# A four-layer streaming encoder on one core: half of the heads' evictions on another engine, the pooling gate's read issued elsewhere, and the convolution's steps reordered

## The chip, the cores and the metric

The kernel runs on one core of a Trainium2 chip. The core has five engines with queues of their own: TensorE (PE in the profile; its weight loads are shown apart as PEld), VectorE (DVE), ScalarE (ACT), GpSimd (POOL) and SyncE (SP), which only issues transfers. PSUM holds what PE writes, in banks of 128 x 512 fp32. The metric is the device time of one execution in microseconds (us); the number quoted is the median of several runs.

## The reference

256 tokens of 1024 channels pass through four layers. Each layer is a token mixer and then an MLP; the mixer is latent attention (MLA) in layers 0 and 3, a convolution module in layer 1 and a pooling mixer in layer 2. All arrays are fp32. Cut to what matters here:

```python
for i in range(DEPTH):                       # 4
    mod = silu(c) @ ada_w[i] + ada_b[i]      # six rows of 1024: shift, scale, gate, twice
    sh_m, sc_m, gt_m, sh_f, sc_f, gt_f = split(mod, 6)
    h = rmsnorm(x, g[i, 0]) * (1 + sc_m) + sh_m
    y = mixer(h)                             # i % 3: 0 MLA, 1 convolution, 2 pooling
    x = x + gt_m * rmsnorm(y, g[i, 1])
    h = rmsnorm(x, g[i, 2]) * (1 + sc_f) + sh_f
    y = square(relu(h @ w1[i])) @ w2[i]      # 1024 -> 4096 -> 1024
    x = x + gt_f * rmsnorm(y, g[i, 3])

def conv(h):
    a = h @ w_pw1 + b_pw1                    # 1024 -> 2048
    u = a[:, :1024] * sigmoid(a[:, 1024:])
    u = causal_depthwise(u, w_dw) + b_dw     # width 31
    return silu(layernorm(u)) @ w_pw2 + b_pw2

def pool(h):                                 # four groups of 256 channels, windows 2, 4, 8, 16
    p = trailing_mean(h) - h
    return (p @ w (by group) + b) * scale
```

## The kernel before

**Tiles.** The tokens are two tiles of 128 (tile 0 and tile 1), the channels eight blocks of 128. The residual stream `xs` stays in SBUF. Every fp32 matrix product is made of three products of rounded parts, high x high, high x low and low x high. For weights `load` brings a raw tile by DMA (issued on SP), ScalarE casts it to `hi` (L173), and VectorE subtracts that from the raw tile, which gives `lo` (L174). The activations are split in the same way: the tile `hT` holds a high and a low plane of the transposed activations.

**Heads.** Between two sublayers stands one call of `boundary` (L536; called a head here). For each token tile it does the following. ScalarE sums the squares of the result `y` (L135), POOL forms the root (L119, L121), VectorE multiplies y by the gate's row `bc_g` (`y_scaled`, L528, giving v) and adds it to the residual (`residual`, L533). `squares` then sums the squares of the new xs on ScalarE (L135, tile ms), POOL forms that root r, and VectorE multiplies xs by the scale row `bc_a` to give `xa`. PE turns xa into hT. For tile 0 that is `transposed0`: ScalarE writes a diagonal `dg` of r (L403), PE adds the shift and multiplies with dg (L395, L409) into two banks of four channel blocks each, and `fill0(h)` empties each bank into the planes, by a cast on ScalarE (L573) and a subtraction on VectorE (L574). For tile 1 it is `transposed1`: xa already holds r (L420), PE transposes (L426), ScalarE and VectorE empty the banks (L429, L431). Between them stands `first(0)`, the first product of the next sublayer with tile 0 (`headblock`, L645); `turned` then does tile 1 and turns the block (L659), which ScalarE copies out first (L657 in the convolution, L728 in the MLP). There are eight heads: six fill planes in this way, the one ahead of the pooling mixer hands over tokens instead, and the last one only writes the output.

**Modulation.** The rows of `mod` are computed in the background, in units of one 1024 x 2048 piece of `ada_w`: `ada(n, vec)` does n units, either on PE (L271, tile adap) or, for those in `vec`, as sums on VectorE (L221, L223, tile acc) that `ada_flush` hands to PE at the end. Tables (`MIX`, `FF`) say how many units each step of a stage does. A finished row is written to DRAM (`stage`), and read back to all partitions by a DMA that POOL issues (`spread`, L331); `gate_row(i)` does that for the gate bc_g, `prep` for bc_a.

**Order.** SP issues in the order in which the program is written. The other engines are ordered by the tile scheduler. `line(eng, ins)` pins an instruction behind the one pinned before it on its engine, and `gate[eng]` names an instruction behind which later weight casts, low parts, adap products or DMA reads are placed, without a semaphore. `gate["free"]` counts how many loads may pass ahead of it.

**Convolution** (`conv`, L1107). In iteration m of eight, PE forms block m of the first projection (`colblock`), ScalarE the sigmoid (L1174), VectorE the gated product `up` (L1176). SP writes that to DRAM (`ud`, L1179) and reads it back spread over shifted rows (`spread_taps`, L1150, four reads, tile u). `taps` runs 32 small matmuls with diagonal weights (L1131, tile dw_ps), ScalarE empties them with the bias (`uc`, L1134), and PE turns the result into tokens (L1136, tile ctok). Blocks 0 to 5 are done inside the loop for both tiles at once; blocks 6 and 7 after it, with the tiles as the outer loop:

```python
            for t in range(NT):
                for p, dg in zip(pend, dgs):
                    taps(*p, dg, t * P, P)
```

Then come the norm of each tile on VectorE (L1204 to L1211), its transposes on PE (L1220), the swish on ScalarE (L1225), the split on VectorE (L1230, L1231) and the second projection (`rowblock`, L602 to L606).

**Pooling** (`pool`, L1265). The head gives it tokens of tile 0 (L1290, on VectorE); its first call of `early` makes the window means of tile 0 on PE (L1309), the second one the first half of the product (L1330). ScalarE and VectorE split the means (L1317, L1320). After the head come tile 0's low product, tile 1's means, the gate's row (`gate_row(i)`) and tile 1's product.

## Time and profile before

| | |
|---|---|
| median of three runs | 1166.6 us (1164.24 to 1167.7) |
| profiled execution, device time | 1165.46 us |
| its span in the trace | 1163.7 us |
| mean granted clock of TensorE | 0.985 of full speed |
| busy in that span: PE, PEld, DVE, ACT, POOL | 1116.9, 910.8, 860.2, 643.3, 55.8 us |
| instructions | 17551, of them 6682 matmuls |
| moved by DMA | 290.02 MB, 249 GB/s in the mean |

The span runs from the first to the last instruction of the profiled execution; the device time beside it is that of the same execution. A row of the trace names the line of the kernel, the engine, the operation, the tile written and those read. A number in square brackets is the time for which the engine stood still just before, with what released it. [...]

### The profile page before, as it was taken

To read this page: it belongs to the slowest core of one execution; us is meant where nothing else is said; L and a number is where in the kernel's file an instruction comes from. 1 tells how busy PE (TensorE), PEld (TensorE's weight loads), DVE (VectorE), ACT (ScalarE), POOL (GpSimd) and SP (SyncE) were. 2 spreads that over 40 slices of the span, in tenths; PEclk is the share of its full clock that TensorE was granted. 3 is DMA by queue.
4 is the path that set the end of the run, shared out by engine and by line. 5 is a ranking of instruction groups with operands and counts; after the bars stand their busy time and mean duration, and the time that the engine had idled before them with its cause. 6 is when DMAs were issued, how large, how long until landed. Compare 5 with 4: busy or idle time off the path is not lost.

```text
span 1163.7 us, 17551 instructions
## 1 busy us (share of the span) xinstructions
PE 1116.9 (96%) x6682; PEld 910.8 (78%) x6682; DVE 860.2 (74%) x1206; ACT 643.3 (55%) x1146; POOL 55.8 (5%) x129
## 2 busy tenths in 40 slices
PE   7899999999999989999999989999998899999997
PEld 4667778878877767888888768888877778888886
DVE  3789788889675656888876688888756986655554
ACT  3455566555654225655564555656556665655653
POOL 1000000000010001000000100000010001000000
PEclk8999999999999989999999989999998999999999
DMA  9877769987825894898877559988625522765650
GB/s 367 321 275 305 294 241 348 336 318 286 316 86 174 308 341 155 307 388 328 307 282 293 226 207 379 332 314 289 210 72 177 172 91 71 258 197 188 188 187 36
DMA packets 73388, 290.02 MB, mean 249 GB/s; under 512 B 9988, under 2 KB 15236, under 8 KB 61016
## 3 DMA queue, kind: packets, MB, share of 16 engines
q1 hardware_dynamic: 70488, 280.45, 66.5%
q0 software_dynamic: 2816, 8.46, 2.1%
q8 instruction: 52, 0.85, 0.3%
q14 instruction: 32, 0.26, 0.1%
HBM read 286.58 MB, written 2.29 MB: 248 GB/s over the span
## 4 chain that ended last, share of the span: by engine, by line
PE 79%; DVE 7%; DMA 6%; ACT 3%; issue 3%; POOL 2%; SPq 0%; POOLq 0%; DVEq 0%; ACTq 0%
PE h L671 19%; PE y L602 11%; PE y L605 11%; PE y L606 11%; PE h L674 10%; PE adap L271 2%; DMA raw<-in_w_pw_dram 2%; ACT junk L135 2%; PE dw_ps L1131 2%; PE s_ps L1043 1%; DVE lo L174 1%; PE h L645 1%; POOL r L121 1%; PE pw L625 1%; PE pw L619 1%
## 5 line engine op out<-in xcount | busy, mean ns | idle before, releaser
L174 DVE TENSOR_TENSOR lo<-raw,hi 128x1024 fp32r<-128x1024 f32 (+1 forms) x334 | 391.4, 1194 | 79.6 <-ACT hi L173 53.1
L173 ACT CAST hi<-raw 128x1024 fp32r<-128x1024 f32 (+1 forms) x334 | 333.8, 1029 | 67.4 <-PE y L606 32.1
L671 PE MATMUL h<-hT,hi 128*128 128x512 f32 x960 | 240.0, 391 | 0.0
L671 PEld LDWEIGHTS h<-hT,hi 128*128 128x128 f32 x960 | 175.9, 188 | 36.2 <-issue 2.5
L605 PE MATMUL y<-lo,gh 128*128 128x512 f32 x512 | 200.0, 391 | 0.1
L606 PE MATMUL y<-hi,gl 128*128 128x512 f32 x512 | 199.1, 390 | 0.0
L602 PE MATMUL y<-hi,gh 128*128 128x512 f32 x512 | 197.2, 393 | 1.4 <-ACT hi L173 1.4
L736 ACT COPY r<-h 128x256 f32<-128x256 f32 x120 | 44.6, 372 | 183.4 <-PE h L674 183.3
L674 PEld LDWEIGHTS h<-hT,lo 128*128 128x128 f32 x960 | 130.8, 190 | 11.5 <-issue 2.5
L223 DVE SCALAR_TENSOR_TENSOR acc<-araw,c_act,acc 128x1024 f32<-128x1024 f32 x110 | 135.8, 1280 | 0.6 <-DMA araw<-in_ada_w_dram 0.5
L674 PE MATMUL h<-hT,lo 128*128 128x256 f32 x960 | 135.0, 283 | 0.0
L606 PEld LDWEIGHTS y<-hi,gl 128*128 128x128 f32 x512 | 96.1, 188 | 21.0 <-DVE gl L742 0.6
L602 PEld LDWEIGHTS y<-hi,gh 128*128 128x128 f32 x512 | 95.6, 188 | 21.2 <-ACT hi L173 1.6
L605 PEld LDWEIGHTS y<-lo,gh 128*128 128x128 f32 x512 | 96.3, 188 | 20.3 <-issue 1.7
L737 DVE TENSOR_TENSOR r<-h,r 128x256 f32<-128x256 f32 x120 | 50.3, 421 | 44.6 <-ACT r L736 43.5
L742 DVE TENSOR_TENSOR gl<-r,gh 128x512 fp32r<-128x512 f32 x60 | 41.4, 691 | 39.5 <-ACT gh L741 39.1
L738 ACT ACTIVATE r<-r 128x512 f32<-128x512 f32 x60 | 38.0, 633 | 33.3 <-DVE r L737 33.0
L528 DVE TENSOR_TENSOR v<-y,bc_g 128x512 f32<-128x512 f32 x32 | 21.9, 688 | 27.0 <-ACT junk L135 20.3
L602 PE MATMUL y<-hi,hT 128*128 128x512 f32 x96 | 38.2, 399 | 1.3 <-DVE hT L1230 1.3
L739 ACT ACTIVATE r<-r 128x512 f32<-128x512 f32 x60 | 37.9, 632 | 1.6
L741 ACT CAST gh<-r 128x512 fp32r<-128x512 f32 x60 | 37.2, 621 | 1.7
L605 PE MATMUL y<-lo,hT 128*128 128x512 f32 x96 | 37.5, 391 | 0.0
(262 smaller groups left out, 1470.2 us busy)
## 6 DMA issues: line engine op xcount, KB each, us to landing
raw<-in_w_dram SPq DMA_DIRECT2D x256, 512.0 KB, 4.7
araw<-in_ada_w_dram SPq DMA_DIRECT2D x96, 1024.0 KB, 7.2
raw<-in_w_pw_dram SPq DMA_DIRECT2D x24, 512.0 KB, 7.5
raw<-in_w_o_dram SPq DMA_DIRECT2D x16, 512.0 KB, 4.4
u<-ud SPq DMA_DIRECT2D x32, 132.0 KB, 3.3
raw<-in_w_ukv_dram SPq DMA_DIRECT2D x8, 512.0 KB
bc_g<-rowd POOLq DMA_DIRECT2D x8, 512.0 KB, 4.2
bc_a<-rowd POOLq DMA_DIRECT2D x7, 512.0 KB, 8.0
```

Of the source, the lines that this page charges most:

```text
L173: put(A.copy(h, raw), "act")
L174: put(V.tensor_tensor(l, raw, h.bitcast(F32), op=ALU.subtract), "dve")
L223: V.scalar_tensor_tensor(acc, raw[:, sl], ck, acc, op0=ALU.mult, op1=ALU.add)
L602: mm = T.matmul(o, ah, bh, start=start, stop=False, skip_group_check=True)
L605: T.matmul(o, ah, bl, start=False, stop=False, skip_group_check=True)
L606: return T.matmul(o, al, bh, start=False, stop=stop, skip_group_check=True)
L671: T.matmul(b, w(0, kk), pair[:, :, kk], start=(kk == 0), stop=False, skip_group_check=True)
L674: T.matmul(b[:, 0:S], w(1, kk), pair[:, 0, kk], start=False, stop=(kk == KT - 1), skip_group_check=True)
L736: A.copy(rf, hb[:, S:])
L737: V.tensor_tensor(rf, hb[:, 0:S], rf, op=ALU.add)
L738: A.activation(r, r, AF.Relu)
L742: gli = V.tensor_tensor(gl, g2, gh.bitcast(F32), op=ALU.subtract)
```

## The change

- In the six heads that fill planes, `fill0(1)` casts on VectorE instead of ScalarE, and it is issued behind tile 1's residual, squares and root. Where the head does modulation units, the first half's low part is issued ahead of it.
- In the head before layer 2's MLP the low parts of the first weight block are `held`: they are placed behind `scaled(0)`.
- In the pooling stage `gate_row(i)` is called in the head's first call of `early`, where it stood behind tile 1's means.
- Modulation sums on VectorE are placed behind `gate["dve"]`.
- In the convolution the turnings of a block are collected and done in the middle of the next taps (`turn`), the reads of block m-1 are issued on SP ahead of block m's write, the last two blocks run with the block as the outer loop, `ada_flush` comes behind them, adap products are placed behind the latest tap matmul, casts from m = 2 on behind the copies of the head block, and `MIX[1]` has its units in another order.

```diff
-    def load(src, pre=None, lined=False):
+    def load(src, pre=None, lined=False, held=None):
...
-        put(V.tensor_tensor(l, raw, h.bitcast(F32), op=ALU.subtract), "dve")
+        def rest():
+            return V.tensor_tensor(l, raw, h.bitcast(F32), op=ALU.subtract)
+        if held is None:
+            put(rest(), "dve")
+        else:
+            held.append(lambda: line("dve", rest()))
...
+                    if gate["dve"] is not None:
+                        nosync(ins, gate["dve"])
...
             xa = scaled(0)
+            for h in held:
+                h()
...
         def fill0(h):
             o = (slice(None), slice(4 * h, 4 * h + 4), slice(0, P))
-            line("act", A.copy(planes[0][o], bs[h]))
+            if h == 0:
+                line("act", A.copy(planes[0][o], bs[h]))
+            else:
+                line("dve", V.tensor_copy(planes[0][o], bs[h]))
             return lambda: line("dve", V.tensor_tensor(
                 planes[1][o], bs[h], planes[0][o].bitcast(F32), op=ALU.subtract))
         if tokens is None:
-            low = [fill0(h) for h in range(2)]
+            low = [fill0(0)]
         residual(1, v1, r1)
...
         else:
+            if units:
+                low.pop(0)()
+            low.append(fill0(1))
             for l in low:
                 l()
...
+            turns = []
+
+            def turn():
+                for uc, m, c0, w in turns:
+                    for t in range(w // P):
+                        line("pe", T.transpose(
+                            ctok[c0 // P + t][m // 4][:, (m % 4) * P:(m % 4) * P + P],
+                            uc[:, t * P:(t + 1) * P], ident))
+                turns.clear()
...
                 for mm in range(8):
+                    if mm == 4:
+                        turn()
                     for q in range(4):
-                        T.matmul(b[32 * q:32 * q + 32, 0:w], dg[:, mm, q, :],
-                                 u4[:, q, mm + c0:mm + c0 + w], start=(mm == 0), stop=(mm == 7))
+                        gate["pe"] = line("pe", T.matmul(
+                            b[32 * q:32 * q + 32, 0:w], dg[:, mm, q, :],
+                            u4[:, q, mm + c0:mm + c0 + w], start=(mm == 0), stop=(mm == 7)))
...
-                for t in range(w // P):
-                    T.transpose(ctok[c0 // P + t][m // 4][:, (m % 4) * P:(m % 4) * P + P],
-                                uc[:, t * P:(t + 1) * P], ident)
+                turns.append((uc, m, c0, w))
...
-                    hb = turned(first, vp.tile([P, 512], F32, tag="uc", name="r0", bufs=2), A.copy)
+                    def put(rt, b):
+                        cpy.append(A.copy(rt, b))
+                    cpy = []
+                    hb = turned(first, vp.tile([P, 512], F32, tag="uc", name="r0", bufs=2), put)
+                    last.clear()
                 else:
+                    if m == 2:
+                        gate["act"] = cpy[1]
                     hb = colblock(w_pw1[j, m], hh, hl, "pw1")
...
+                if m > 0:
+                    pend.append(spread_taps(*uds.pop(0)))
                 ud = dr.tile([4, 32, 288], F32, tag="ud", name="ud")
                 nc.sync.dma_start(ud.rearrange("b r t -> (b r) t"), u)
                 uds.append((m, ud))
-                if m > 0:
-                    pend.append(spread_taps(*uds.pop(0)))
...
-            ada_flush()
...
-            for t in range(NT):
-                for p, dg in zip(pend, dgs):
+            for p, dg in zip(pend, dgs):
+                for t in range(NT):
                     taps(*p, dg, t * P, P)
+            turn()
+            ada_flush()
...
             if not spilt:
+                gate_row(i)
                 parts = [means(0, h) for h in range(2)]
...
         gate["free"] = 0
-        gate_row(i)
         prep(i, 2)
...
-        1: ([0, 0, 2, 1, 2, 1, 1, 0, 0], 1, 3),
+        1: ([0, 1, 2, 1, 2, 1, 0, 0, 0], 1, 3),
...
-                first = headblock(w1[i, 0] if m else w_pw1[i // 3, 0], hi, lo)
+                held = [] if m and i % 3 == 2 else None
+                first = headblock(w1[i, 0] if m else w_pw1[i // 3, 0], hi, lo, held)
```

The lines of the changed kernel differ: fill0's cast is L583 on ScalarE and L585 on VectorE, the low part L586, dg L410, the transposes' evictions L436, xa L427, the taps L1159, the turnings L1147, the write of ud L1214, the reads of u L1177.

**ScalarE in the head ahead of layer 1's MLP.** The squares with tile msy are those of y, with ms those of the new xs; dg is tile 0's diagonal; L573 (now L583) empties tile 0's banks, L429 (now L436) those of tile 1; L728 and L729 (now L743 and L744) begin the MLP's first block. Before:

```order
L135 ACTIVATE junk,msy<-y_4485 128x512
L403 ACTIVATE dg<-ident,r 128x128
L135 ACTIVATE junk,msy<-y_4486 128x512
L573 CAST hT<-hT_ps 128x4x128 x2
L135 ACTIVATE junk,ms<-xs 128x512 x2
L728 ACTIVATE r<-h_4709 128x256
L429 ACTIVATE hT<-hT_ps,shc 128x128 x4
```

and now:

```order
L135 ACTIVATE junk,msy<-y_4485 128x512
L410 ACTIVATE dg<-ident,r 128x128
L135 ACTIVATE junk,msy<-y_4486 128x512
L583 CAST hT<-hT_ps 128x4x128
L135 ACTIVATE junk,ms<-xs 128x512 x2
L743 ACTIVATE r<-h_4709 128x256
L436 ACTIVATE hT<-hT_ps,shc 128x128 x8
```

One of the two casts has left ScalarE, and the squares of tile 1's xs follow the first cast directly; the copy of the MLP's block now stands ahead of all of tile 1's evictions. On VectorE the second cast stands between the two low parts, behind tile 1's residual (L540) and ahead of xa.

**VectorE in the pooling stage,** from the split of the means on. L1320 (now L1354) is the low part of the means, L528 (now L535) y times the gate's row, L533 (now L540) the residual, L389 (now L396) xa of tile 0, L174 (now L175) the low part of a weight. Before:

```order
L1320 TENSOR_TENSOR hT<-pT_ps,hT 128x4x128
L528 TENSOR_TENSOR v<-y_6499,bc_g 128x512
L528 TENSOR_TENSOR v<-y_6500,bc_g 128x512
L1320 TENSOR_TENSOR hT<-pT_ps,hT 128x4x128 x2
L174 TENSOR_TENSOR lo<-raw,hi 128x1024 x2
L533 SCALAR_TENSOR_TENSOR xs<-v,r,xs 128x512 x2
L389 TENSOR_TENSOR xa<-xs,bc_a 128x512 x2
L528 TENSOR_TENSOR v<-y_6501,bc_g 128x512
```

and now:

```order
L1354 TENSOR_TENSOR hT<-pT_ps,hT 128x4x128
L535 TENSOR_TENSOR v<-y_6501,bc_g 128x512
L535 TENSOR_TENSOR v<-y_6502,bc_g 128x512
L540 SCALAR_TENSOR_TENSOR xs<-v,r,xs 128x512
L1354 TENSOR_TENSOR hT<-pT_ps,hT 128x4x128 x2
L540 SCALAR_TENSOR_TENSOR xs<-v,r,xs 128x512
L396 TENSOR_TENSOR xa<-xs,bc_a 128x512 x2
L175 TENSOR_TENSOR lo<-raw,hi 128x1024 x2
L535 TENSOR_TENSOR v<-y_6503,bc_g 128x512
```

The two weight low parts have moved behind tile 0's residual and xa, and the residual's halves stand around the low parts of tile 1's means.

**TensorE at the end of the convolution,** from block 6's taps for tile 0 on. The operand u_4192 (now u_4188) is block 6, u_4236 (now u_4234) block 7; ctok_3392 is the second channel half of tile 0's tokens, ctok_3394 that of tile 1. Before:

```order
L1131 MATMUL dw_ps<-u_4192,dg 32x128 x32
L1136 MATMUL ctok_3392<-ident,uc 128x128
L1131 MATMUL dw_ps<-u_4236,dg 32x128 x32
L1131 MATMUL dw_ps<-u_4192,dg 32x128 x5
L1136 MATMUL ctok_3392<-ident,uc 128x128
L1131 MATMUL dw_ps<-u_4192,dg 32x128 x27
L1131 MATMUL dw_ps<-u_4236,dg 32x128 x5
L1136 MATMUL ctok_3394<-ident,uc 128x128
L1131 MATMUL dw_ps<-u_4236,dg 32x128 x27
L1220 MATMUL sT_ps<-ident,un 128x128 x4
L1136 MATMUL ctok_3394<-ident,uc 128x128
```

and now:

```order
L1159 MATMUL dw_ps<-u_4188,dg 32x128 x32
L1147 MATMUL ctok_3392<-ident,uc 128x128
L1159 MATMUL dw_ps<-u_4188,dg 32x128 x16
L1159 MATMUL dw_ps<-u_4234,dg 32x128 x16
L1147 MATMUL ctok_3394<-ident,uc 128x128
L1159 MATMUL dw_ps<-u_4234,dg 32x128 x32
L1147 MATMUL ctok_3392<-ident,uc 128x128
L1159 MATMUL dw_ps<-u_4234,dg 32x128 x16
L278 MATMUL adap<-acc,ones_c 32x512 x3
L1147 MATMUL ctok_3394<-ident,uc 128x128
L278 MATMUL adap<-acc,ones_c 32x512
L1254 MATMUL sT_ps<-ident,un 128x128 x8
```

Tile 0's tokens were complete while 59 tap matmuls of tile 1 were still to come; they are now complete 16 tap matmuls before the taps end.

## Rows read from the trace of the kernel before

**Rows 1.** The page, part 1: busy time of each engine, share of span, instructions.
```profile
span 1163.7 us, 17551 instructions
PE 1116.9 (96%) x6682; PEld 910.8 (78%) x6682; DVE 860.2 (74%) x1206; ACT 643.3 (55%) x1146; POOL 55.8 (5%) x129
```
**Rows 2.** Waits of PE, whole span: who waits, on whom; us in total, times, longest.
```profile
PE hT_ps L426 <- DVE xa L420: 6.6, 11, 1.9
...
PE y L1330 <- DVE hT L1320: 2.9, 1, 2.9
PE ctok L1136 <- ACT uc L1134: 2.7, 5, 1.1
...
PE dw_ps L1131 <- DMA u<-ud: 2.0, 1, 2.0
...
PE gT L659 <- ACT r L657: 1.1, 1, 1.1
```
**Rows 3.** Windows: us, busy of PE, PEld, DVE, ACT, POOL, PEclk, DMA share, GB/s.
```profile
346.00:352.00 6.00, 4.87 (x42) 4.67 (x41) 5.98 (x14) 5.74 (x11) 0.55 (x1) 1.00 0.28 90
423.60:429.60 6.00, 5.42 (x93) 4.69 (x97) 0.00 (x0) 0.37 (x1) 0.00 (x0) 0.51 0.96 384
655.00:670.00 15.00, 12.62 (x100) 10.93 (x92) 7.20 (x12) 6.75 (x14) 3.38 (x7) 1.00 0.99 399
873.60:876.40 2.80, 2.78 (x12) 2.78 (x13) 1.54 (x6) 2.14 (x8) 0.55 (x1) 0.50 0.79 291
```
**Rows 4.** Timeline, head of layer 1's MLP: start, us, instruction, [wait before, releaser].
```profile
467.97 0.59 ACT L573 CAST hT<-hT_ps 128x512 fp32r<-128x512 f32 x1 [0.91 <-PE hT_ps L409]
468.45 0.64 ACT L135 ACTIVATE junk<-xs 128x512 bf16<-128x512 f32 x1
...
467.09 0.69 DVE L574 TENSOR_TENSOR hT<-hT_ps,hT 128x512 fp32r<-128x512 f32 x1 [0.81 <-ACT hT L573]
...
471.01 1.54 DVE L420 SCALAR_TENSOR_TENSOR xa<-xs,r,bc_a 128x256 f32<-128x256 f32 x3 [1.73 <-POOL r L121]
...
471.55 0.83 PE L426 MATMUL hT_ps<-ident,xa 128*128 128x128 f32 x4 [0.75 <-DVE xa L420]
```
**Rows 5.** Groups by line and form: busy us, mean ns of one, idle before, releaser.
```profile
L1067 DVE COPY ptA<-pT_ps 128x512 f32<-128x512 f32 x8 | 5.5, 691 | 2.3 <-PE pT_ps L1066 2.2
...
L573 ACT CAST hT<-hT_ps 128x512 fp32r<-128x512 f32 x12 | 7.0, 587 | 14.2 <-PE hT_ps L409 14.2
...
L223 DVE SCALAR_TENSOR_TENSOR acc<-araw,c_act,acc 128x1024 f32<-128x1024 f32 x110 | 135.8, 1280 | 0.6 <-DMA araw<-in_ada_w_dram 0.5
```
**Rows 6.** Timeline, pooling stage, columns as in rows 4.
```profile
654.82 0.68 DVE L528 TENSOR_TENSOR v<-y,bc_g 128x512 f32<-128x512 f32 x1
...
659.77 0.63 POOL L331 DMA_DIRECT2D bc_g<-rowd  x1
...
668.54 1.29 DVE L528 TENSOR_TENSOR v<-y,bc_g 128x512 f32<-128x512 f32 x2 [6.67 <-DMA bc_g<-rowd]
...
670.94 2.35 DVE L174 TENSOR_TENSOR lo<-raw,hi 128x1024 fp32r<-128x1024 f32 x2
...
670.48 1.33 PE L1330 MATMUL y<-hi,hT 128*128 128x256 f32 x8 [2.86 <-DVE hT L1320]
...
684.31 0.90 PE L426 MATMUL hT_ps<-ident,xa 128*128 128x128 f32 x4
685.46 0.63 PE L426 MATMUL hT_ps<-ident,xa 128*128 128x128 f32 x4 [0.25 <-DVE xa L420]
```
**Rows 7.** Tile bc_g, its DMA reads from issue to landing.
```profile
DMA to landing us min/median/max: 3.8/4.2/8.7
```
**Rows 8.** Timeline, end of the convolution, columns as in rows 4 (SPq: SyncE's queue).
```profile
417.36 4.61 SPq L1150 DMA_DIRECT2D u<-ud  x8
...
431.69 0.70 DVE L1204 BATCH_NORM_STATS2 st<-ctok 128x6 f32<-128x512 f32 x1 [8.26 <-PE ctok L1136]
...
438.75 0.50 PE L602 MATMUL y<-hi,hT 128*128 128x512 f32 x1 [1.33 <-DVE hT L1230]
```

More of the change, by code (lines that the diff above doesn't have):

```diff
@@ L220, in ada @@
                     if first:
-                        V.tensor_scalar(acc, raw[:, sl], ck, None, ALU.mult)
+                        ins = V.tensor_scalar(acc, raw[:, sl], ck, None, ALU.mult)
                     else:
-                        V.scalar_tensor_tensor(acc, raw[:, sl], ck, acc,
-                                               op0=ALU.mult, op1=ALU.add)
+                        ins = V.scalar_tensor_tensor(acc, raw[:, sl], ck, acc,
+                                                     op0=ALU.mult, op1=ALU.add)
+                    if gate["dve"] is not None:
+                        nosync(ins, gate["dve"])
             else:
@@ L534, in residual, with boundary @@
                                                op0=ALU.mult, op1=ALU.add))
-    def boundary(ys, units, planes=None, tokens=None, early=None, first=None):
+    def boundary(ys, units, planes=None, tokens=None, early=None, first=None, held=()):
         defer[0] = []
@@ L627, in colblock, with headblock @@
         return b
-    def headblock(src, hh, hl):
-        parts = [load(src[p]) for p in range(2)]
+    def headblock(src, hh, hl, held=None):
+        parts = [load(src[p], held=held) for p in range(2)]
         banks = []
@@ L1406, in tile_trunk @@
             hi, lo = planes()
-            first = None
+            first = held = None
             if m or i % 3 == 1:
-                first = headblock(w1[i, 0] if m else w_pw1[i // 3, 0], hi, lo)
+                held = [] if m and i % 3 == 2 else None
+                first = headblock(w1[i, 0] if m else w_pw1[i // 3, 0], hi, lo, held)
             elif s:
@@ L1416, in tile_trunk @@
             else:
-                head(planes=(hi, lo), first=first and first[0])
+                head(planes=(hi, lo), first=first and first[0], held=held or ())
             if m:
```

## The prediction

> **What bounds the kernel now.** I read the page's first part first: TensorE (PE) is busy for 1116.9 us of a span of 1163.7 [rows 1]. The number of matmuls does not change, so what the change can win lies in the 46.8 us in which PE stands still, and in stretches where it works at its lower clock. The view of waits for PE alone [rows 2] tells who makes it stand still: in the six heads (the function boundary) it waits 6.6 us, 11 times, for VectorE's product xa; in the pooling stage 2.9 us for VectorE's low part hT; in the convolution 2.7 us for uc, 2.0 us for the spread copy u, 1.1 us for r. The windows [rows 3] give the second part. [...] Inside the MLPs PE has no such waits, so what a stage wins or loses moves all behind it.
>
> **Part 1, five heads: squares before the second eviction.** The layer 1 head shows the step [rows 4]. ScalarE's cast of the second half starts at 467.97, since it waits for PE's second bank; the squares of tile 1 stand behind it and start at 468.45. They feed POOL's root; xa starts when that is done, at 471.01, and PE, which had stood 0.75 us since tile 0's last product at 470.8, starts tile 1's transposes at 471.55. Tile 1's residual stands ahead of the low part in VectorE's order, and the first cast was over when that low part began at 467.09. So squares, root and xa can come 1.4 us sooner (468.45 less some 467.06). The cast goes to VectorE, which is free from 467.78 on: it starts when the bank is full, about 467.95.
>
> The cast's price on VectorE is in no row for this tile. A copy of the same size out of PSUM takes 691 ns there, ScalarE's cast takes 587 [rows 5]; I take 0.69, as that row has the same source, size and engine. [...]
>
> With 0.69 the second half's high part is there at 468.65, its low part at 469.35, and xa can start at 469.6: PE, which ends tile 0 at 470.8, finds the first pieces ready. The wait for xa goes. Two small ones take its place: PE may reach the second half before the cast ends (0 to 0.6 us, I take 0.3, since VectorE comes from the residual), and ScalarE reaches the copy of tile 1's block later by its weight casts (0 to 0.5, I take 0.3 in the MLP heads of layers 0, 1 and 3). Of the 6.6 us of waiting [rows 2], 0.25 [rows 6] is the pool's. So: 6.35 - 5 x 0.3 - 3 x 0.3 = **3.9 us**, between 1.9 (all eight at their ends) and 6.3. In the head into layer 3 the longest single wait, 1.9 us, breaks into pieces under 0.7; nearest are the waits of about 1.1 that left the clock at 1.00, so the 2.8 us at half clock go: **1.4 us**, at least 0.
>
> **Part 2, the pooling stage.** The chain is plain [rows 6]. POOL issues the read of the gate's row bc_g at 659.77, VectorE stands 6.67 us for it until 668.54, with two low parts of hT, which do not need it, queued behind. PE waits 2.86 us for those until 670.48; two weight low parts (2.35 us from 670.94) stand before the residual. PE comes to tile 1's transposes at 684.31, and stands 0.25 us before the second four. Issued in the head's first call of early, the read can start when VectorE has last used the old row, at 655.5 (654.82 and 0.68). This kind of read takes 3.8 to 8.7 us, median 4.2 [rows 7]: it lands between 659.5 and 664.3. The longest is nearest, for the same transfers are in flight: from 655 to 670 the DMA engines are busy 0.99 [rows 3]. VectorE then goes on at 664.3 at the latest, where it went on at 668.54. Then: products 664.3 to 665.6, one residual half 666.3, both low parts 667.6 (PE hardly waits), the other half 668.3, xa 669.6 if bc_a is in by 668.5, held weights 672.0, row 1's products and residual 675.1, low, cast, low 677.1. PE does its product, adap and transposes by 673.3, the first half's high part by 674.3, then waits some 2 us for the cast at 676.4, and is through tile 0 at 678.4: 5.9 us sooner than 684.31. That wait is as long as those after which the clock fell, so I take off 1.4: **4.5 us**. Bounds: 6.2 (no such wait, no clock lost) and 2.5 (the read lands as late as the slowest and half clock for twice as long).
>
> **Part 3, the convolution.** What can go [rows 2, 3]: 2.7 us for uc, since the turnings now stand in the middle of the next taps; 2.0 us for u, as the read of block 6 no longer stands behind the write of block 7: SP issued the eight reads from 417.36 on [rows 8], the first four could have gone some 5 us sooner; the half clock after it, 5.4 us of work [rows 3], so 2.7; of the 1.1 us for r about half, as two weight casts instead of three stand before that copy: 0.5. Together 7.9. What comes: block by block, tile 0 is only complete after block 7's first half is turned, in the middle of PE's last taps. From its statistics to the first product it is 7.1 us now (431.69 to 438.75 [rows 8]), of which PE held back the transposes by about 1.9; so 5.2, in which PE has the rest of the taps (1 us), the last adap, 0.5, and eight transposes, 0.8. It waits some 2.9 us instead of 1.3, and I count half clock after it, 1.4 as in part 1's row, since it is longer than the waits that kept it. 7.9 - 1.6 - 1.4 = **4.9 us**; bounds 6.3 (clock kept) and 1.4 (block 7's read late by 1 us, block 5's uc late by 1 behind two weight casts, and 3 us more at half clock, 1.5). The ada units move one iteration earlier: I cost them at nothing: no PE wait of this stage names their sums [rows 2]. If that cover is gone, it is one unit of two passes of 1280 ns [rows 5] in front of a low part.
>
> **The sum.** 3.9 + 1.4 + 4.5 + 4.9 = 14.7 us. The profiled execution took 1165.46 us, 1.8 outside the span and 1.1 under the median of 1166.6. 1165.46 - 14.7 = 1150.8; I write **1151**.
>
> **The rivals.** *The gate lands no sooner.* From 655 to 670 the transfers asked for keep the DMA engines full [rows 3], and a read issued 4 us earlier may only wait in that crowd: the 8.7 us read against a median of 4.2 [rows 7] speaks for it; against it, the row's read then has POOL's queue for itself. Part 2 falls to the held weights and the low parts placed before the second residual half, about 1 us: 1154.3.
>
> *New waits eat half.* [...] What the rows say is that waits of 1.9 and 2.0 us were followed by half clock [rows 2, 3]. If the heads give 1.9 and no clock back, and the waits at the pool's cast and before the second projection leave those stages at their lower bounds, 2.5 and 1.4, the time is 1165.5 - 5.8 = 1159.7.
>
> *Slower: VectorE late in every head.* The cast stands behind tile 1's residual and, where the head has ada units, the first low part. It decides when the cast starts 2.0 us or more after PE wants the second half: with 1.4 lost to the clock each, the five heads then cost 17, all that is won (6.3 + 1.4 + 4.5 + 4.9 = 17.1). At 2.9 us a head, as PE stood in the pool, they cost 21.5, and the pool's head 0.9 more than counted: 5.3 slower, 1171. For it: I reckon such a wait in the pool's head. Against it: in layer 1 VectorE stands free for 0.8 us before the second half's low part [rows 4].
>
> *Hidden.* What PE waits for could be set by something that the rows name only last, a landing of weights; then nothing moves, 1165. Against it: the releasers are VectorE and ScalarE nearly everywhere.
>
> **How the numbers follow.** The forecast 0.62, its own range 1146 to 1156. The gate no sooner 0.14, new waits 0.14, slower 0.04, hidden 0.06. About 0.3% (3.5 us) is what a measurement can tell from no change. The first three are faster by more, 0.90; hidden is the same, 0.06; slower 0.04. The upper ends together are 6.3 + 1.4 + 6.2 + 6.3 = 20.2, 1145; the runs shown lie up to 2 us apart from the profiled one, so 1144. Above, the range reaches to the new-waits case, 1160.
>
> **What would show it.** Right: the waits for xa under 2 us in all; squares starting right behind the first cast; no wait for bc_g on VectorE, and PE's product in the pool without one; no wait for uc or for block 6's u, clock 1.00 through the last taps, a longer wait before the second projection. Wrong: PE standing in each head for the cast; VectorE still waiting for bc_g near 668; half clock through the second projection.

## The result, and the profile after

The changed kernel takes **1155.67 us** (median of 4 runs, 1153.88 to 1157.11) where the kernel before takes 1166.16 (4 runs beside it): a ratio of 0.9913, 95% interval 0.9892 to 0.9933, or 10.1 us less (7.8 to 12.6). The forecast was 1151, with a range of 1144 to 1160.

The page of the profiled execution, part 1, as in [rows 1]:

```profile
span 1155.0 us, 17554 instructions
PE 1115.2 (97%) x6682; PEld 912.7 (79%) x6682; DVE 865.0 (75%) x1212; ACT 638.6 (55%) x1140; POOL 57.3 (5%) x129
```

The span is 8.7 us shorter and PE's busy time 1.7, so most of what was won is standstill: 39.8 us are left of 46.8. The six casts show as 6 instructions more on VectorE and 6 fewer on ScalarE. The waits of PE, over the whole span, as in [rows 2]:

```profile
PE hT_ps L416 <- ACT dg L410: 2.6, 2, 2.0
...
PE dw_ps L1159 <- issue: 1.8, 1, 1.8
...
PE y L617 <- DVE hT L1264: 1.6, 1, 1.6
...
PE dw_ps L1159 <- DMA u<-ud: 1.2, 3, 0.6
PE dw_ps L1159 <- DVE up L1209: 1.0, 1, 1.0
PE hT_ps L433 <- DVE xa L427: 0.9, 3, 0.5
...
PE h L660 <- DVE hT L585: 0.4, 1, 0.4
PE gT L674 <- ACT r L1198: 0.4, 1, 0.4
```

and one line of that list before, which [rows 2] does not show:

```profile
PE hT_ps L409 <- ACT dg L403: 2.0, 2, 1.4
```

The wait for hT in the pooling stage is down to 0.2 us and that for uc has gone, as forecast; of the 6.6 us for xa 0.9 are left. The wait for dg, the diagonal, in the pool's head has grown from 1.4 to 2.0 us, and 4.0 us stand in the convolution's taps (1.8, 1.2 and 1.0), where the forecast's sum has none.

Where the time went shows best by stretch, in us. The table is worked out from the timelines: each stretch runs from the first matmul of one kind to the first of the next. The last three columns are kernels with one part of the change alone (next section).

| us from ... to ... | before | changed | heads | gate | conv. |
|---|---|---|---|---|---|
| start, to the first head | 147.33 | 150.93 | 149.18 | 149.07 | 150.83 |
| layer 0's MLP: head, with tile 0's product | 13.18 | 12.85 | 12.88 | 13.16 | 13.18 |
| the rest, to the next head | 177.13 | 176.78 | 176.78 | 177.05 | 177.10 |
| convolution: head | 13.05 | 10.73 | 12.38 | 13.04 | 11.79 |
| to the first taps | 13.20 | 13.40 | 13.20 | 13.20 | 12.75 |
| first taps to second projection | 74.86 | 72.91 | 70.68 | 70.85 | 72.92 |
| second projection | 26.11 | 26.12 | 26.13 | 26.13 | 26.14 |
| layer 1's MLP: head | 13.18 | 12.30 | 12.30 | 13.18 | 13.16 |
| the rest | 177.58 | 177.25 | 177.22 | 177.58 | 177.58 |
| pooling, to the head's transposes | 19.67 | 15.31 | 19.68 | 15.42 | 19.63 |
| layer 2's MLP: head (the pool's) | 15.57 | 15.83 | 15.27 | 14.72 | 15.80 |
| the rest | 174.34 | 174.04 | 174.00 | 174.56 | 174.35 |
| layer 3's attention: head, to the first pT | 53.11 | 50.44 | 51.06 | 52.59 | 52.91 |
| the rest | 56.32 | 57.80 | 57.80 | 57.82 | 57.83 |
| layer 3's MLP: head | 13.23 | 12.40 | 12.40 | 13.20 | 13.21 |
| the rest | 175.84 | 175.91 | 175.94 | 175.83 | 175.82 |

Two rows are no effect of the change. The start, which it leaves alone, is 3.6 us longer in this execution; over the 14 profiles of this study it lies between 147.3 and 152.4. The rest of layer 3's attention is 1.48 longer because of the clock (last section). Of the others, the heads and the pooling stage are shorter, about as forecast, and so is the convolution's long stretch, by 1.95 us. That last number hides a loss: the same old loop takes 70.7 and 70.9 us in the kernels with the heads or the gate alone.

The head of layer 1's MLP, timeline, as in [rows 4]:

```profile
465.33 0.59 ACT L583 CAST hT<-hT_ps 128x512 fp32r<-128x512 f32 x1 [2.52 <-PE hT_ps L416]
...
465.81 0.63 ACT L135 ACTIVATE junk<-xs 128x512 bf16<-128x512 f32 x1
...
466.82 0.69 DVE L585 CAST hT<-hT_ps 128x512 fp32r<-128x512 f32 x1 [0.19 <-PE hT_ps L416]
...
468.37 1.54 DVE L427 SCALAR_TENSOR_TENSOR xa<-xs,r,bc_a 128x256 f32<-128x256 f32 x3
...
469.59 1.04 PE L433 MATMUL hT_ps<-ident,xa 128*128 128x128 f32 x8
```

The squares start 0.48 us behind the start of the first cast. VectorE's cast takes 0.69 us and waits 0.19 for the bank. xa follows the low parts without a gap, and PE runs into tile 1's transposes without one.

The pooling stage and the pool's head, timeline, as in [rows 6]:

```profile
653.45 0.63 POOL L338 DMA_DIRECT2D bc_g<-rowd  x1 [0.27 <-DVE v L535]
...
662.86 1.29 DVE L535 TENSOR_TENSOR v<-y,bc_g 128x512 f32<-128x512 f32 x2 [3.34 <-DMA bc_g<-rowd]
...
665.46 1.33 PE L1364 MATMUL y<-hi,hT 128*128 128x256 f32 x8 [0.19 <-DVE hT L1354]
...
667.81 2.35 DVE L175 TENSOR_TENSOR lo<-raw,hi 128x1024 fp32r<-128x1024 f32 x2
...
667.58 1.53 POOL L119 TENSOR_SCALAR v<-ms 128x1 f32<-128x1 f32 x1 [4.77 <-ACT junk L135]
669.20 1.39 POOL L121 TENSOR_TENSOR r<-v,mhalf 128x1 f32<-128x1 f32 x1
...
671.07 1.16 PE L416 MATMUL hT_ps<-dg,xa 128*128 128x128 f32 x8 [2.01 <-ACT dg L410]
```

VectorE's wait for the gate's row has halved (6.67 to 3.34), PE's wait for hT is down from 2.86 to 0.19. What is new stands below: POOL's two instructions for tile 0's root take 1.53 and 1.39 us, beside VectorE's two held low parts, and PE stands 2.01 us for dg. The pooling stage and the pool's head together, columns as in [rows 3] (PEclk is the granted clock as a share of full speed, in the mean over the stretch), in the kernel before, the changed one and the one with the gate alone:

```profile
655.62:690.86 35.24, 30.63 (x205) 24.71 (x202) 22.91 (x39) 18.95 (x45) 5.75 (x12) 0.90 0.67 261
```

```profile
653.27:684.41 31.14, 28.94 (x207) 24.95 (x204) 23.58 (x40) 18.02 (x44) 7.82 (x12) 0.95 0.77 293
```

```profile
653.26:683.40 30.14, 27.39 (x205) 23.03 (x202) 22.73 (x39) 18.94 (x45) 7.22 (x12) 1.00 0.79 304
```

Of the 4.1 us that the changed kernel takes less here, 2.4 are standstill of PE and 1.7 its busy time, which is the clock: in the kernel before it lies at its lower level twice, from 671.8 to 675.2 (0.51) and from 678.7 to 682.1 (0.50), in the changed one once, behind the wait for dg (0.53 from 672.16 to 675.66), and with the gate alone not at all (1.00). The forecast does not name these stretches of the kernel before. The three other profiles with the gate's old place also have 6.8 us at the lower level here.

### The profile page after: what moved, and what is told of

Its sections match the earlier page's. It is cut to its first block, busy times and chain, and to the rows that moved or that the text cites. A ratio compares the mean times of both kernels' runs of the same rounds, so it can differ in the third digit from the quotient of the medians.

```text
span 1155.0 us, 17554 instructions
## 1 busy us (share of the span) xinstructions
PE 1115.2 (97%) x6682; PEld 912.7 (79%) x6682; DVE 865.0 (75%) x1212; ACT 638.6 (55%) x1140; POOL 57.3 (5%) x129
## 4 chain that ended last, share of the span: by engine, by line
PE 79%; DVE 7%; DMA 7%; issue 3%; ACT 2%; POOL 2%; SPq 1%; POOLq 0%; DVEq 0%; ACTq 0%
PE h L686 19%; PE y L617 11%; PE y L620 11%; PE y L621 11%; PE h L689 10%; PE adap L278 2%; PE h L660 2%; DMA ud<-up 2%; PE s_ps L1058 1%; DVE lo L175 1%; ACT junk L135 1%; DMA raw<-in_w_pw_dram 1%; POOL r L121 1%; DMA bc_g<-rowd 1%; DMA bc_a<-rowd 1%
## 5 line engine op out<-in xcount | busy, mean ns | idle before, releaser
L175 DVE TENSOR_TENSOR lo<-raw,hi 128x1024 fp32r<-128x1024 f32 (+1 forms) x334 | 391.8, 1193 | 84.4 <-ACT hi L173 57.0
L535 DVE TENSOR_TENSOR v<-y,bc_g 128x512 f32<-128x512 f32 x32 | 21.9, 688 | 23.2 <-ACT junk L135 19.8
```

Of the source, the lines that this page charges most:

```text
L175: return V.tensor_tensor(l, raw, h.bitcast(F32), op=ALU.subtract)
```

## The experiments

**The parts alone.** Three kernels are the kernel before with one part of the change, taken from its diff: `heads_only` has the new `fill0` and its calls, `gate_only` the moved `gate_row(i)`, `conv_only` everything else but `held`. The fourth, `squares_first`, tells engine from order: it has the new order, with both casts on ScalarE.

The edit of `heads_only`, against the kernel before:

```diff
-            line("act", A.copy(planes[0][o], bs[h]))
+            if h == 0:
+                line("act", A.copy(planes[0][o], bs[h]))
+            else:
+                line("dve", V.tensor_copy(planes[0][o], bs[h]))
...
-            low = [fill0(h) for h in range(2)]
+            low = [fill0(0)]
...
+            if units:
+                low.pop(0)()
+            low.append(fill0(1))
```

`squares_first` has its last two pieces only. The edit of `gate_only`:

```diff
             if not spilt:
+                gate_row(i)
...
         gate["free"] = 0
-        gate_row(i)
```

> The kernel before with part 1 alone: in the six heads that fill planes the second half's cast is on VectorE, behind tile 1's residual and squares. Theory (the prediction's part 1): PE's waits for xa fall from 6.6 us to under 1.5 and the low clock after the head into layer 3 goes, 5.3 us faster, 1.9 to 7.7. Rival (new waits eat it): PE waits for the cast in each head, 0 to 2 us faster. In the changed kernel's profile the five heads apart from the pool's are 7.0 us shorter together, so if the parts add up this is 5 to 7 us faster.

> As heads_only, but the second half's cast stays on ScalarE, behind the squares of tile 1's residual. Theory order: what paid was that the squares no longer stand behind a cast that waits for PE; the cast then starts some 0.6 us later than on VectorE, xa comes as early, so within 1 us of heads_only. Theory engine: freeing ScalarE of the cast paid; then less than half of what heads_only gives, with PE waiting for the second half's cast (0.5 to 1.5 us in each head).

> The kernel before with the gate's row read from the head's first call of early, nothing else. Theory (part 2): the read lands by 664.3 or sooner where it landed at 668.5, VectorE and PE's product go on earlier; 2.5 to 5 us faster, the second projection of the wait for hT (2.9 us) gone. Rival (gate no sooner, the transfers in flight hold it): under 1 us. The weights' low parts stand here ahead of the residual, as before: if they matter as in the prediction, the gain is 1 us under that of the whole part.

> The kernel before with the convolution's part alone (turnings, reads ahead of the write, blocks outer, units, adap products behind the taps, sums behind the gate). Theory (part 3): 4.9 us faster, 1.4 to 6.3. Rival, from the changed kernel's profile: PE stands 1.8 us for nothing that the profile shows in the last taps, just as an instruction fetch (queue 8) lands among full DMA engines, 1.0 us at block 4's taps and 1.2 us in three waits for u, so that 2 to 3 us are left; if these are part of the change and not of that one execution, they are seen here again at the same places.

| kernel | median us | ratio to before (95%) | us less |
|---|---|---|---|
| heads_only | 1158.87 | 0.9939 (0.9926 to 0.9952) | 7.1 |
| squares_first | 1160.1 | 0.9951 (0.9933 to 0.9968) | 5.7 |
| gate_only | 1161.27 | 0.9960 (0.9947 to 0.9974) | 4.7 |
| conv_only | 1165.26 | 0.9993 (0.9975 to 1.001) | 0.8 |

(Us less is 1 less the ratio, times 1166.2.) The heads give more than forecast, the gate as much, the convolution nothing that can be told from zero. The waits for xa of `heads_only`, and below them those of `squares_first`:

```profile
PE hT_ps L426 <- DVE xa L420: 1.3, 4, 0.7
...
PE h L651 <- DVE hT L576: 0.4, 1, 0.4
```

```profile
PE h L648 <- ACT hT L573: 2.3, 4, 0.7
...
PE hT_ps L426 <- DVE xa L420: 1.5, 3, 1.1
```

So most of part 1 is order: the squares no longer stand behind a cast that waits for PE. The engine shows in the other line: PE waits 2.3 us in all for the second cast where that is on ScalarE, and 0.4 where it is on VectorE. In the whole time the two kernels lie within 1.4 us, and their intervals overlap, so that the times alone do not show what the engine is worth.

**What the convolution's change costs.** The stretch from the first taps to the second projection, windows view, one line each of the kernel before, `heads_only` (both old loop) and the changed kernel (new loop):

```profile
363.89:438.75 74.86, 68.59 (x921) 52.87 (x920) 42.55 (x47) 23.13 (x37) 4.00 (x8) 0.95 0.83 287
```

```profile
364.42:435.10 70.68, 66.12 (x921) 50.93 (x920) 42.53 (x47) 23.02 (x37) 4.04 (x8) 1.00 0.87 297
```

```profile
364.69:437.60 72.91, 67.80 (x921) 50.93 (x921) 43.70 (x48) 23.02 (x36) 4.19 (x8) 1.00 0.89 290
```

At full clock the old loop is the faster one here, by 2.2 us, and of those PE's busy time is 1.7 (66.12 to 67.80). One pair says little, since the waits differ from profile to profile: at full clock the old loop took 70.7, 70.9 and 71.4 us (`heads_only`, `gate_only`, `squares_first`), the new one 72.9, 72.9, 71.1 and 73.8 (the changed kernel, `conv_only`, and `held_late` and `held_act`, below, which leave it as it is). The kernel before had lost its clock there (0.95 over 74.86 us) in the execution that was profiled. At full clock the old loop has the waits of [rows 2], only shorter; in `heads_only`:

```profile
PE ctok L1142 <- ACT uc L1140: 1.5, 3, 0.7
...
PE dw_ps L1137 <- DMA u<-ud: 1.2, 1, 1.2
```

Five kernels look for the reason: `conv_back` puts the whole loop back, `turn_now` and `flush_early` one step each, `combo` those two together (with `held_late`, below), and `less_dma` takes transfers away.

`conv_back` is the convolution of the kernel before, but with the changed copies of the head's block (`put`, `last.clear()` and `cpy[1]`) and with the sums behind `gate["dve"]`. The edits of `turn_now` and `flush_early`, against the changed kernel:

```diff
-                    if mm == 4:
-                        turn()
...
                 turns.append((uc, m, c0, w))
+                turn()
...
-            turn()
```

```diff
             wp = [load(w_pw2[j, k]) for k in range(4)]
+            ada_flush()
...
             turn()
-            ada_flush()
```

and that of `less_dma`, cut to the transfer. It leaves out seven eighths of five transfers, and the instructions that read these tiles read the 256 columns repeatedly, so that its output is not the reference's:

```diff
+            if (i, g) == (2, 0) and k < 5:
+                nc.sync.dma_start(raw[:, 0:256], ada_w[i, g, k][:, 0:256])
+            else:
+                nc.sync.dma_start(raw, ada_w[i, g, k])
...
```

> The changed kernel with the convolution's loop, reads, last blocks, turnings and units as before; only the copies of its head block keep the new order. New theory: the change to the convolution's loop costs time, since without the half clock that the profile of before happens to have there, the stretch from the first taps to the second projection takes 70.7 us with the old loop and 72.9 with the new one. Then this kernel is 1 to 3 us faster than the changed one, some 12 to 13 us faster than before (1153 to 1154). Rival (the prediction's part 3): the new loop saves 4.9 us, and this kernel is that much slower than the changed one, 5 to 6 us faster than before.

> The changed kernel with each block's turnings directly behind its taps, as before. Theory of the prediction: waits for uc of 1.5 to 2.7 us come back, the stretch is 74.5 to 75.5 instead of 72.9. Rival: the loop's pace is set by its transfers (the DMA engines are busy 0.87 to 0.89 of it), waits for u shrink by what uc costs, and breaking the taps cost PE 1.1 us of busy time; then the stretch stays within 0.7 us of 72.9.

> The changed kernel with the sum's adap products ahead of the last taps, as before. Theory: at the end they stand between the last taps and tile 0's transposes, which start 1.5 us after their input is ready; ahead, the transposes and the second projection start about 1 us sooner, so the stretch from the first taps to the second projection is 72 instead of 72.9. Rival: PE waits there for VectorE's norm in any case, nothing moves.

> The changed kernel, but five units of layer 2's first modulation rows bring only 256 of their 2048 columns, which are used eight times; this leaves out the rest of those rows and 3.5 MB of the transfers of the convolution's loop, while every engine does the same instructions. Theory transfers: the loop's waits ahead of taps (1.0 to 1.8 us at block 4, 0.4 to 1.2 for u, 0.4 to 1.8 for nothing shown) are late transfers; they shrink to under 1 us in all and the stretch takes 69 to 70 us instead of 71.1 to 72.9. Rival: the waits are VectorE's or the queue's own order; the stretch stays at 71 to 73.

| kernel | first taps to second projection, us | time, us |
|---|---|---|
| conv_back | 71.78, clock low once | 1155.5 (0.9914, 0.9891 to 0.9937) |
| turn_now | 70.05 | 1154.81, one run |
| flush_early | 71.38 | 1152.59, one run |
| combo | 74.00 | 1155.65 (0.9919, 0.9892 to 0.9947) |
| less_dma | 70.32 | 1153.58, one run |

`conv_back` is as fast as the changed kernel. Neither expectation came true: the new loop neither costs 1 to 3 us in the median nor saves 4.9. `turn_now` fell below both bounds that were set for it, and `combo`, with the same turnings, came out 4 us longer: the stretch scatters by some 4 us with waits that move. In `combo` they are these, of which the second is the one at block 4's taps:

```profile
PE ctok L1147 <- ACT uc L1161: 3.8, 5, 1.4
PE dw_ps L1157 <- DVE up L1208: 2.2, 1, 2.2
```

That wait is put down to the product `up` of block 6, but it is a transfer's. The changed kernel and `less_dma`, PE and VectorE at block 4's taps:

```profile
406.75 1.51 PE L1159 MATMUL dw_ps<-u,dg 128*32 128x256 f32 x24 [1.03 <-DVE up L1209]
```

```profile
404.29 1.96 PE L1170 MATMUL dw_ps<-u,dg 128*32 128x256 f32 x32
...
404.90 0.48 DVE L1220 SCALAR_TENSOR_TENSOR up<-pw,cv_b,sg 128x256 f32<-128x256 f32 x1 [1.41 <-ACT sg L1218]
```

In `less_dma`, and likewise in `turn_now`, these taps begin 1.1 us before the same product ends, so they do not need it. What they read are the four reads of block 4, in the changed kernel issued on SP as:

```profile
393.55 1.91 SPq L1177 DMA_DIRECT2D u<-ud  x4
```

These were issued ahead of the write of block 5 (397.70), as planned, and the last of them reports its end at 406.55, some 13 us after the first was issued. PE starts 0.20 us later, and it does so in all seven profiles that have this wait. With 4.6 MB fewer to bring, `less_dma` has the DMA share of the stretch down from 0.89 to 0.76:

```profile
363.31:433.63 70.32, 67.44 (x921) 50.46 (x920) 43.74 (x49) 23.32 (x37) 4.19 (x8) 1.00 0.76 241
```

The four reads then end 7.7 us after the first was issued, and PE waits neither for `up` nor for u. (One profile does not show that fewer transfers were needed for it: in `turn_now`, with all of them, the reads ended after 11.2 us, just in time.) What is left of PE's waits there:

```profile
PE y L628 <- DVE hT L1275: 1.6, 1, 1.6
PE dw_ps L1170 <- issue: 1.3, 1, 1.3
```

So late transfers make the waits ahead of the taps; the one without a shown releaser they don't explain. It stands in the last taps of all kernels with the new loop that keep the turnings in the taps (1.82, 1.45, 0.42, 0.69, 1.26 and 1.74 us), and shorter in `heads_only` (0.26), `squares_first` (0.46) and `combo` (0.35). In all nine profiles one packet of the queue that brings instructions starts 2.2 to 2.4 us ahead of the end of the wait, however long that is. In the changed kernel, where the wait ends at 432.43, the DMA queues from 430.0 to 430.5 show:

```profile
q8 instruction: 1, 0.02, 11.0%
```

That PE stands there for its next instructions is likely, but not shown: no run moved that fetch.

The other cost is in PE's own time. Lines and forms of that stretch, `heads_only` and then the changed kernel:

```profile
L1137 PE MATMUL dw_ps<-u,dg 128*32 128x256 f32 x384 | 22.1, 381 | 0.0
...
L271 PE MATMUL adap<-acc,ones_c 128*32 128x512 f32 x16 | 2.1, 604 | 0.0
```

```profile
L1159 PE MATMUL dw_ps<-u,dg 128*32 128x256 f32 x384 | 23.2, 383 | 1.6 <-DVE up L1209 1.0 <-DMA u<-ud 0.6
...
L278 PE MATMUL adap<-acc,ones_c 128*32 128x512 f32 x16 | 3.2, 600 | 0.0
```

The same matmuls, each as long as before, cover 1.1 us more where the turnings break a run of taps, and 1.1 more where the adap products stand apart. The single steps confirm both: in `turn_now` the taps are back at 22.1 and the adap products still at 3.2, in `flush_early` it is 23.2 and 2.1, in `combo` 22.1 and 2.1. PE's busy time in the whole stretch is 67.4 to 67.8 in the five kernels that have both steps and 65.4 to 66.1 in the three at full clock with the old loop and in `turn_now`, `combo` and `combo_act`. So the new order costs PE about what the waits for uc were worth (1.5 in `heads_only`).

**The pool's head.** `held_late` moves the held low parts behind tile 1's first product with the gate's row; `combo_act` and `held_act` also give that head's second cast back to ScalarE. `combo` and `combo_act` have `turn_now` and `flush_early` besides.

Against the changed kernel, `held_late`, and then what `held_act` and `combo_act` have besides:

```diff
             xa = scaled(0)
-            for h in held:
-                h()
...
         v1 = [y_scaled(1, ys, 0)]
+        for h in held:
+            h()
```

```diff
-            if h == 0:
+            if h == 0 or held:
                 line("act", A.copy(planes[0][o], bs[h]))
...
-            low = [fill0(0)]
+            low = [fill0(h) for h in range(2 if held else 1)]
...
-            low.append(fill0(1))
+            if not held:
+                low.append(fill0(1))
```

> The changed kernel with the two held low parts of weights placed behind tile 1's first product with the gate's row instead of ahead of it. Theory port: in the pool's head POOL's two instructions for the root took 1.53 and 1.39 us where they take 0.30 and 0.56 elsewhere, since VectorE's subtractions (two operands in SBUF) ran beside them; PE stood 2.0 us for dg. Behind the product the root is done some 2 us sooner: the wait for dg under 0.5, the pool's head 2 us shorter, 3.7 with the half clock that followed. Rival: POOL's root is late for another reason (its input), and nothing moves.

> The changed kernel with held_late, turn_now and flush_early together. If what each showed alone adds up: the stretch from the first taps to the second projection 70 us (72.9 in the changed kernel's profile, 71.1 to 72.9 over its loop's runs), the pool's head 14.5 instead of 15.8, so some 3 us faster than the changed kernel, 1152 to 1153, 13 us faster than before. Rival: turn_now's 70.05 was chance, the stretch is 71 to 73 again and only the 1.3 of the pool's head is left, 1154.5.

> combo with the second half's cast of the pool's head alone back on ScalarE, ahead of the squares. In held_late PE stood 1.8 us there for that cast, since VectorE came to it 2 us late, from the held low parts and tile 1's residual; ScalarE stood idle. Theory: the wait goes (under 0.4) and the pool's head is 1.0 to 1.5 us shorter than combo's, more if a half clock follows combo's wait. Rival: the wait moves to VectorE's low part or to xa and nothing is won.

> The changed kernel with the held low parts behind tile 1's first product and, in that head alone, the second half's cast on ScalarE; the convolution as in the changed kernel. From the stretches seen: pool's head 13.9 us (15.8 to 17.5 in the kernels with the changed kernel's head, 13.9 in combo_act), convolution's stretch 71.1 to 72.9; so 2 to 3.5 us faster than the changed kernel, 1152 to 1153.5, 12 to 14 us faster than before. Rival: what the pool's head gives is lost to the clock later, as the low stretch in layer 3's attention comes and goes with the time at which waits fall; then within 1 us of the changed kernel.

Timeline of `held_late`, the same instructions as in the changed kernel:

```profile
663.06 0.54 POOL L119 TENSOR_SCALAR v<-ms 128x1 f32<-128x1 f32 x1 [5.06 <-ACT junk L135]
663.68 0.56 POOL L121 TENSOR_TENSOR r<-v,mhalf 128x1 f32<-128x1 f32 x1
...
664.73 1.16 PE L416 MATMUL hT_ps<-dg,xa 128*128 128x128 f32 x8 [0.18 <-ACT dg L410]
...
669.39 0.68 DVE L585 CAST hT<-hT_ps 128x512 fp32r<-128x512 f32 x1
...
670.13 0.39 PE L660 MATMUL h<-hi,hT 128*128 128x256 f32 x1 [1.79 <-DVE hT L585]
```

POOL's root is down to 0.54 and 0.56 us, and the wait for dg to 0.18: as the expectation from VectorE's subtractions has it, and not as its rival. The next wait shows at once, 1.79 us for VectorE's cast. With that cast on ScalarE it goes too (`held_act`, waits of PE in this stage):

```profile
PE hT_ps L433 <- DVE xa L427: 0.8, 2, 0.5
...
PE hT_ps L416 <- ACT dg L410: 0.2, 1, 0.2
```

The pool's head takes 15.8 to 17.5 us in the five kernels that have it as the changed one does (15.83, and 15.86, 17.49, 17.34 and 17.33 in `conv_back`, `turn_now`, `flush_early` and `less_dma`, the last three with twice as long at the lower clock, in `less_dma` at 0.50 from 668 to 674), 14.51 in `held_late` and 15.81 in `combo` (at 0.50 from 678 to 680), 13.88 in `combo_act` and 13.91 in `held_act`.

| kernel | median us | ratio to before (95%) |
|---|---|---|
| held_late | 1154.36 | 0.9906 (0.9887 to 0.9924) |
| combo_act | 1153.76 | 0.9911 (0.9885 to 0.9936) |
| held_act | 1154.35 | 0.9908 (0.9882 to 0.9934) |

The gain in the stage is plain, the gain in the whole is not: none of the three can be told from the changed kernel (0.9913). `held_act` met the long version of the convolution's stretch (73.76 us) in its profile, and the expected 1152 to 1153.5 did not come.

## Why the prediction was right, and where it was not

The time lies in the range and in the forecast's own, 1146 to 1156. Part of that is luck: of the three parts one gave more than forecast, one as much, and the third next to nothing. Alone they add to 12.6 us, the whole kernel gave 10.1; the intervals allow for the difference.

- **Part 1, forecast 5.3 with the clock, alone 7.1 (5.6 to 8.6).** The mechanism was right: squares behind the first cast, xa ahead of PE's need. The cast at 0.69 was right (686 ns on average). The small waits that were to take the old one's place were taken as 2.4 us in all (5 x 0.3 and 3 x 0.3); the changed kernel's list has 1.7 (0.4 for the cast, 0.4 for a low part in the head into layer 3, 0.9 for xa), so 0.7 too much was taken off. Not counted were the MLPs of layers 0 to 2 behind their heads, which are 0.35 us shorter each in `heads_only`. On ScalarE the cast takes 586 ns here, so the move costs a tenth of a microsecond a cast, which is small against the 5.7 us that the order gives with both casts on ScalarE (`squares_first`). The 1.4 us for the clock in the head into layer 3 were a chance and not a sum: `gate_only` has the same wait of 1.9 us for xa there, and behind it the clock stays at the higher level:

```profile
866.30:869.10 2.80, 2.50 (x17) 2.19 (x17) 2.00 (x9) 2.56 (x9) 0.55 (x1) 1.00 0.82 285
```

- **Part 2, forecast 4.5; the gate alone 4.7 (3.0 to 6.2).** The mechanism was right. The read landed later than the bound taken: the pooling stage begins 2.35 us sooner (653.27 for 655.62), so the 664.3 of the text is 661.9 in this trace, and VectorE went on at 662.86. The read took 9.3 us from issue, where 8.7 was the longest before, so it was slowed, and still came 3.3 us sooner than before. The forecast wait of 2 us in the pool's head and the half clock behind it came, but at another place: for dg, since POOL's root takes 1.53 and 1.39 us beside the held low parts, and not for the cast, which comes to light only when that is mended. The gain of about 1 us ascribed to holding the low parts is not seen: the pool's head takes 14.72 us in `gate_only`, without holding and with both casts on ScalarE, and 15.83 here, and moving the held parts away took the wait for dg with it (`held_late`, 14.51; `combo`, 15.81 with the clock low once). The lower bound of 2.5 comes to 3.1 by the terms that the text names. That a wait of some 2 us costs 1.4 us of clock, as this sum and that of part 3 have it, no run shows: 1.9 us for xa left the clock at 1.00 in `gate_only`, 2.0 for dg was followed by 0.53 here, and 2.06 for p by either (last section).
- **Part 3, forecast 4.9; alone 0.8 (-1.2 to 2.9).** This is the step that failed, "7.9 - 1.6 - 1.4". Of the 7.9, the 2.7 for uc was won and for the most part paid back in PE's busy time (1.7), which the sum put at nothing. The 2.0 for u did not go: the reads were issued sooner and landed in the same crowd, where the waits at the taps of blocks 0, 4, 6 and 7 came to 2.3 us (0.59, 1.03, 0.30 and 0.35). The 2.7 for the half clock was counted as certain and was a chance: with the old order of the reads the clock fell behind the wait for u in two of five profiles (the kernel before and `conv_back`, waits of 2.0 and 1.6 us) and not in three (1.2, 1.3 and 1.5). In the nine profiles with the reads ahead of the write it did not fall in this stretch, not even behind waits of 2.2 and 2.3 us at block 4; whether that is the order or chance is open. The head of the convolution and the way to the first taps gave more than the 0.5 counted: 1.7 us in `conv_only` (26.25 to 24.54), of which the wait for r is 0.9. That is about what the loop lost against the old one at full clock, which fits the 0.8 in the whole. The 1.6 us more of waiting ahead of the second projection did not come: 1.6 in all, where 1.3 stood before, and no half clock after it (1.00).

Of the rivals, "the gate lands no sooner" is excluded by `gate_only`, and "hidden" by the 10.1 us. New waits did eat what part 3 was to give, but the whole is more than the 5.8 us of that rival. The slower one, VectorE late in every head, fell in the heads but is visible in one: the pool's, once the wait for dg is taken away.

## What to carry to other kernels

When an instruction stands behind one that waits, put the one that can go first ahead; that alone gave 5.7 of the 7.1 us of part 1. Here a wait that was to go from a stretch in which the DMA engines were 0.83 to 0.90 busy (the kernel before and `combo`) came back as a wait for a transfer, so look at the DMA share of the stretch before counting such a wait as won. An order that removes a wait can cost the engine itself, as PE here 1.7 us: compare its busy time over the stretch too. And before a half clock is put into a sum as a gain, see whether the same code has it in a second profile.

## What the runs showed of the hardware

**POOL's small instructions stretch beside VectorE's subtractions.** The two that form a root take 0.30 and 0.56 us elsewhere in these stages, and 1.53 and 1.39 beside the two low parts (lo from raw and hi, both in SBUF, 667.81 to 670.16 in all); in `gate_only`, where the same low parts run beside them, 1.44 and 0.85. In the changed kernel the first ends at 669.11, just behind the end of the first low part (669.03), and the second at 670.59, 0.4 us behind that of the second. Moving the low parts away took most of the stretch with it (0.54 and 0.56 in `held_late`). That it is a port, as the expectation of `held_late` calls its theory, no run shows.

**The same wait is followed by either clock.** In layer 3's attention PE waits 2.06 us for p in both kernels. Windows behind that wait, the kernel before and the changed one:

```profile
920.20:924.00 3.80, 3.78 (x33) 3.45 (x35) 3.71 (x6) 2.01 (x3) 0.00 (x0) 1.00 0.56 192
```

```profile
910.80:914.80 4.00, 4.00 (x21) 4.00 (x22) 3.91 (x6) 1.51 (x3) 0.00 (x0) 0.57 0.58 196
```

One keeps the higher level, the other falls to the lower for most of the stretch and loses 1.7 us there (0.43 of 4.00). The change does nothing in that stage. Of the 14 profiles, which all have this wait, eight are at the lower level there for a time (`combo`, `combo_act` and `less_dma` at 0.50 to 0.66) and six are not. In the kernel before the clock also fell behind a wait of 1.42 us (0.50 from 897.1 to 900.0), where the changed kernel has the same wait and stays at 1.00, and in `conv_back` in the head into layer 3, where no wait before it is longer than 0.7 us. So the length of a wait does not by itself tell whether the clock falls behind it, and a forecast can take such a loss only as a chance.
